# adaLN steps in locked groups with one load each, started behind the RWKV scan, and mLSTM scores copied out of PSUM, in a hybrid DiT layer

## The chip, the cores and the metric

One core of a Trainium2 chip runs the whole layer as one program. The metric is the device time of one execution in microseconds (us); lower is better. TensorE multiplies, VectorE (DVE), ScalarE (ACT) and GpSimd (POOL) work elementwise, SyncE (SP) issues most of the DMA transfers. Each engine works through its own queue in the order in which the program lists it.

## What is computed

One layer of a diffusion backbone on 256 latent and 256 context tokens of width 2048, in fp32. The condition vectors c and c_ctx give, through one matrix w_mod of 2048 x 12288, six modulation vectors (adaLN). Cut to what matters here:

```python
mod_x = (silu(c) @ w_mod + b_mod)[:, None, :]
mod_c = silu(c_ctx) @ w_mod + b_mod
sh1x, sc1x, gt1x, sh2x, sc2x, gt2x = split(mod_x, 6)
ux = modulate(rms_norm(x, norm_g[0]), sh1x, sc1x)      # and uc from ctx
s = split_cols(ux @ w_in)                               # also for uc
ya = conv_module(s[0]);  yb = mlstm(s[1], s[2], s[3])
yc = gated_deltanet(s[4], s[5], s[6]);  yd = rwkv7(s[7])
mx = sum(sigmoid(gates) * stack([ya, yb, yc, yd]) @ w_br) @ w_out
x = x + gt1x * rms_norm(mx, norm_g[1])
fx = conv_ffn(modulate(rms_norm(x, norm_g[2]), sh2x, sc2x))
x = x + gt2x * rms_norm(fx, norm_g[3])
```

The recurrent branches scan the context first, then the latents. The modulation of the first norm (sh1, sc1) is needed at the start, gt1 only after the output projection, sh2 and sc2 only before the FFN, gt2 at the end. The mLSTM has four heads; for each, its scores are k against q, 512 keys by 256 queries, which the decay masks then weigh.

## The kernel before

**Big products.** A weight matrix comes in pieces of 256 rows by 512 columns (512 KB, tile `raw`). `load_split` (L187) loads a piece, ScalarE makes its rounded copy `hi` (L198) and VectorE the rest `lo` (L200); TensorE then takes three products per tile. `mode_b` (psum `psB`) keeps weights stationary, `mode_a` (psum `psA`) keeps activations stationary: 12 matmuls of 128x512 per piece for two token tiles. All matmuls are issued in `mm`, L79, so one line holds them all, and the psum's name tells them apart.

**The adaLN product.** `wmod_steps` (L248) makes one block of 512 columns of `mod` in eight steps. A step loads 512 KB of w_mod into the tile `wraw` of the pool `wmr`, which has one buffer, and issues four fp32 matmuls `psw` (two records each in the trace) that add into one PSUM bank. Then ScalarE copies the sums to `wrows` (L268), and two matmuls `psf` spread them; for the blocks of the gains G1 and G2, which hold gt1 and gt2 times a norm's weight on all partitions, VectorE adds the bias to them (L278, from `wbg`, two loads of 256 KB) and GpSimd multiplies. `mod_feed` lists the blocks: first 8 blocks of sh2 and sc2 (`mod2`), then 4 of G1, then 4 of G2. The blocks of sh1 and sc1 are made in phase 0, at the start, and the G2 blocks in the FFN; both use the ring `raw` instead of `wraw`.

**When the steps are issued.** `feed` is called once per piece of `mode_a` and `mode_b`; it adds `rate` to a counter and issues as many steps as the counter has passed. The rate is 0.55 from the mLSTM's columns on (L1578) through `conv_columns`, the gate columns and `gates`; `feed(96)` (L1596) issues what is left of the first 96 steps (12 blocks). The order of the engines' queues is not that of the code: the tile framework schedules the program by a timeline of its own (`schedule_with_timeline_sim`, L1678), so that steps and column pieces fill in where scans wait. A group of instructions under `manual_schedule` stays together.

**Stages in time.** Phase 0 (norm, sh1 and sc1) to about 134 us, RWKV columns and features to 470, the RWKV scan with columns as filling to about 782, then the dense stage: columns, the RWKV output (psum `psgo`, `psyo`), the DeltaNet scan (`gd_scan`), the gate columns. `ml_scan` (L1175) runs from about 1210 to 1318: per head four matmuls of scores into two PSUM banks `psq`, mask matmuls `psr`, the weighted scores `mA` on VectorE and ScalarE (L1247 to L1267), then `psn` (mA against mv), and a division `mlh` (L1271). The auxiliary psums share three banks (`auxg`, L1584). From 1318 the merges of the four branches follow (`merge`, L1324, with `sig` tiles reloaded from DRAM), the convolution module's norm (`pscm`, `pscv`), `out_proj`, and from 1504 the FFN.

**Memory.** Pools are opened and closed in stack order from both sides of SBUF. `wmr` is opened early (L1565), `gop`, the DeltaNet's output, on the right side before `gd_scan`. `G1` (the tile of `g1p`) is opened behind `ml_scan`.

Of the kernel before, what the change touches and what calls it, by code (L numbers as in the profile page):

```python
# [11 lines left out]
F32 = mybir.dt.float32  # L12
# [8 lines left out]
P = 128  # L21
# [20 lines left out]
class Kern:  # L42
# [205 lines left out]
    def wmod_steps(self, cb, dst, raws=None, gain=None):  # L248


        nc, A = self.nc, self.A
        if raws is not None and cb in (0, 4):
            ps = self.mmp.tile([P, 512], F32, tag="mm", name="psw")
        else:
            ps = (self.evp if self.wap is not None else self.aux)("psw")
        w = A["w_mod"][0]
        for j in range(8):
            wr = raws or self.wmr
            raw = self.raw() if wr is None else wr.tile([P, 2, 512], F32, tag="wraw", name="wraw")
            nc.sync.dma_start(out=raw, in_=w[256 * j : 256 * j + 256, 512 * cb : 512 * cb + 512].rearrange("(k p) c -> p k c", p=P))  # L260
            for k in range(2):
                for h in range(2):
                    r = slice(64 * h + 32 * k, 64 * h + 32 * k + 32)
                    self.mm(ps[r, 0:256], self.cst[:, 2 * j + k, :], raw[:, k, 256 * h : 256 * h + 256], start=(j == 0), stop=(j == 7))
            if j < 7:
                yield
        rows = self.stage("f3", 256, "wrows")
        nc.scalar.activation(rows, ps[:, 0:256], AF.Copy)  # L268
        if gain is not None:

            bg = self.stage("f2", 512, "wbg"), self.stage("f2", 512, "wbg")
            for t, row in zip(bg, (A["b_mod"][0], gain)):
                c0 = 512 * cb if row is not gain else 512 * (cb % 4)
                nc.sync.dma_start(out=t, in_=row[c0 : c0 + 512].unsqueeze(0).to_broadcast([P, 512]))
            ps = (self.evp if self.wap is not None else self.aux)("psf")
            for h in range(2):
                self.mm(ps[:, 256 * h : 256 * h + 256], self.selb[:, h], rows)
            nc.vector.tensor_tensor(dst, ps, bg[0], ALU.add)  # L278
            nc.gpsimd.tensor_tensor(dst, dst, bg[1], ALU.mult)
            yield  # L280
            return
        ps = (self.evp if self.wap is not None and raws is None else self.aux)("psf")
        for i in range(2):
            self.mm(ps[:, 4 * i : 4 * i + 4], rows[:, P * i : P * i + P], self.sel4.rearrange("p h c -> p (h c)"))
        n = dst.shape[2]
        bm = self.PC["b_mod"][:, 4 * cb : 4 * cb + 4].unsqueeze(2).to_broadcast([P, 4, n])
        for h in range(2):
            nc.vector.tensor_tensor(dst[:, 2 * h : 2 * h + 2], ps[:, 0:8].rearrange("p (i h c) -> p h i c", h=2, c=2)[:, h, :, 0:n],
                                    bm[:, 2 * h : 2 * h + 2], ALU.add)
        yield  # L290
# [564 lines left out]
    def conv_module(self):  # L855
        nc, PC = self.nc, self.PC
        cp = self.cvp
        cpad = cp.tile([P, 4, 286], F32, name="cpad")
        nc.gpsimd.memset(cpad[:, :, 0:15], 0.0)
        nc.gpsimd.memset(cpad[:, :, 271:286], 0.0)  # L860
        nc.sync.dma_start(out=cpad[:, :, 15:271], in_=self.dcv)
        acc = cp.tile([P, 4, 256], F32, name="cacc")
        w = lambda i, t: PC["conv_dw"][:, 4 * t + i : 4 * t + i + 1]
        for i in range(4):
            a = acc[:, i]
            nc.vector.tensor_scalar(a, cpad[:, i, 0:256], w(i, 0), PC["conv_b"][:, i : i + 1], ALU.mult, ALU.add)
            for t in range(1, 31):
                nc.vector.scalar_tensor_tensor(a, cpad[:, i, t : t + 256], w(i, t), a, ALU.mult, ALU.add)  # L868
        ps = self.aux("pscm")
        for i in range(4):  # L870
            self.mm(ps[:, 0:256], self.ones, acc[:, i], start=i == 0, stop=i == 3)
        mean = cp.tile([P, 256], F32, tag="cmean", name="cmean")
        nc.scalar.activation(mean, ps[:, 0:256], AF.Copy, scale=1.0 / 512)
        ps2 = self.aux("pscv")
        for i in range(4):
            nc.vector.tensor_tensor(acc[:, i], acc[:, i], mean, ALU.subtract)
            sq = cp.tile([P, 256], F32, tag="ctap", name="csq", bufs=2)
            nc.scalar.activation(sq, acc[:, i], AF.Square)
            self.mm(ps2[:, 0:256], self.ones, sq, start=i == 0, stop=i == 3)
        rt = cp.tile([P, 256], F32, tag="cmean", name="crt")  # L880
        nc.scalar.activation(rt, ps2[:, 0:256], AF.Sqrt, bias=self.eps6, scale=1.0 / 512)
        nc.vector.reciprocal(rt, rt)
        for i in range(4):
            nc.vector.tensor_tensor(acc[:, i], acc[:, i], rt, ALU.mult)
            nc.scalar.activation(acc[:, i], acc[:, i], AF.Silu, bias=PC["conv_ln_b"][:, i : i + 1], scale=PC["conv_ln_g"][:, i : i + 1])
        self.dbg("ya", acc)
        for i in range(4):
            self.put_y(0, i, acc[:, i])
# [120 lines left out]
        for off, ev, t0, n in ((C_GDK, ev_k, 0, 512), (C_GDV, ev_v, 0, 512), (C_GDQ, ev_q, 256, 256)):  # L1009
            self.mode_b(self.win(off, 512), 512, [(P * i, P, t0, n, ev(i)) for i in range(4)], self.uh, self.ul, KT)  # L1010

    def gd_scan(self):
        nc = self.nc
        gp = self.bp
        ges = ExitStack()
        up = self.pool("gup", stack=ges, side="right")
        wp = self.pool("gwp", bufs=2, stack=ges, side="right")
        tp = self.pool("gtp", stack=ges, side="right")
        lg, beta = self.lg, self.beta
        b4 = lambda ap, r=P: ap.unsqueeze(2).to_broadcast([r, 4, P])  # L1020

# [9 lines left out]
        for c in range(2):  # L1031
            r = slice(64 * c, 64 * c + 64)
# [30 lines left out]
        for seg in range(2):  # L1063
# [5 lines left out]
            for jj in range(2):  # L1069
                j = 2 * seg + jj  # L1070
# [12 lines left out]
                for h in range(4):  # L1083
                    for c in range(2):
                        r = slice(64 * c, 64 * c + 64)
# [11 lines left out]
            for i in range(4):  # L1097
# [21 lines left out]
                if seg:  # L1119

                    g = go[:, (0, 1, 1, 0)[i]]
                    pq = v4(self.aux("pQS"))
# [20 lines left out]
        for c in range(2):  # L1143
            r = slice(64 * c, 64 * c + 64)
# [30 lines left out]
    def ml_scan(self):  # L1175
        nc = self.nc
        self.mlx = ExitStack()
        mp = self.pool("mrp", stack=self.mlx)
        wa = self.pool("mwa", bufs=2, stack=self.mlx)
        wp = self.pool("mwb", bufs=2, stack=self.mlx)  # L1180
        qk = self.pool("mqk", stack=self.mlx)
        mqT, mkT = qk.tile([P, 4, 256], F32, name="mqT"), qk.tile([P, 4, 512], F32, name="mkT")
        mv = mp.tile([P, 4, 4, 132], F32, name="mv")
        nc.gpsimd.memset(mv[:, :, :, 128:129], 1.0)
        nc.sync.dma_start(out=mqT, in_=self.dmq)
        nc.sync.dma_start(out=mkT, in_=self.dmk)
# [6 lines left out]
        for d in range(2):  # L1193
            li, lf, b, m = (mp.tile([4, 512], F32, tag="mr%d" % k, name="mr%d" % k) for k in range(4))
            for src, dst in ((self.li, li), (self.lf, lf)):
                ps = self.aux("psml")
# [12 lines left out]
            ps = self.aux("psmt")  # L1209
# [8 lines left out]
            r = mp.tile([4, 256], F32, name="mlr%d" % d)  # L1218
# [17 lines left out]
        for h in range(4):  # L1236
            pq = [self.aux("psq%d" % i) for i in range(2)]
            for j in range(4):
                self.mm(pq[j // 2][:, 256 * (j % 2) : 256 * (j % 2) + 256], mkT[:, h, P * j : P * j + P], mqT[:, h])
            for d in range(2):  # L1240
                pr = self.aux("psr")
                self.mm(pr[:, 0:256], sel[:, h], rr[d])
# [295 lines left out]
    def build(self):  # L1538
# [12 lines left out]
        ues = self.ues = ExitStack()  # L1551
        self.up = self.pool("up", stack=ues)
        bp = self.bp = self.pool("bp", stack=ues)
        self.wmr = self.pool("wmr", bufs=1, stack=ues)
        self.xes = ExitStack()
        self.x2 = self.pool("x2", stack=self.xes)
        fes = ExitStack()
# [17 lines left out]
        self.aux_pool("auxr", u=2, s=1)  # L1575
        self.rw_scan()
        self.gd_columns()
        self.rate = 0.55  # L1578
        self.ml_columns()
        self.conv_columns()  # L1580
        self.gz = self.gate_columns(C_GDZ, AF.Silu, "gz")
# [3 lines left out]
        res.close()  # L1585
        ces = ExitStack()
        cvs = ExitStack()
        self.cvp = self.pool("cvp", stack=cvs, side="right")
        self.gop = self.pool("gop", stack=ces, side="right")
        self.gd_scan()  # L1590
        self.gd_out()
        ces.close()
        self.ml_scan()
        self.G[0] = self.pool("g1p", stack=ues).tile([P, D], F32, name="G1")
        self.gates()
        self.feed(96)  # L1596
        self.rate = 0.0
# [3 lines left out]
        self.dbg("yh", self.uh[:, :, 0:256].bitcast(F32))  # L1601
        self.dbg("yl", self.ul[:, :, 0:256].bitcast(F32))
        self.resp = self.pool("resp", side="right")
        self.hlp = self.pool("hlp", bufs=2, stack=ues)
        self.mgw = self.pool("mgw", bufs=3, stack=ues)
        self.mgp = self.pool("mgp", stack=ues)
        self.mg = self.mgp.tile([P, 2, D], F32, name="mg")
        self.x1 = self.resp.tile([P, 2, D], F32, name="x1")
        self.ffdw = self.resp.tile([P, 404], F32, name="ffdw")
        self.nc.sync.dma_start(out=self.ffdw[:, 0:396], in_=self.A["taps"])  # L1610
# [71 lines left out]
```

## Time and profile before

| | |
|---|---|
| runs (three) | 2315.18, 2315.31, 2319.65 us |
| median | 2315.31 us |
| profiled execution | 2316.15 us, its span 2313.7 us |
| TensorE busy | 2216.0 us, 96% of the span |
| VectorE, ScalarE, GpSimd busy | 1448.9, 990.7, 374.2 us |
| chain of work that ended last | TensorE 83%, VectorE 6%, DMA 5% |
| DMA | 471.97 MB, mean 204 GB/s |

The profile is of one execution. Its stretches are given in us from the span's start. A piece "x8" in the timeline is eight records in a row of one kind; the time in square brackets is how long the engine stood before it, and for what. A busy TensorE may still run at the lower of its two clocks; the granted clock is given per stretch as a share of the full one.

### The profile page before, as it was taken

To read this page: it belongs to the slowest core of one execution; us is meant where nothing else is said; L and a number is where in the kernel's file an instruction comes from. 1 tells how busy PE (TensorE), PEld (TensorE's weight loads), DVE (VectorE), ACT (ScalarE), POOL (GpSimd) and SP (SyncE) were. 2 spreads that over 40 slices of the span, in tenths; PEclk is the share of its full clock that TensorE was granted. 3 is DMA by queue.
4 is the path that set the end of the run, shared out by engine and by line. 5 is a ranking of instruction groups with operands and counts; after the bars stand their busy time and mean duration, and the time that the engine had idled before them with its cause. 6 is when DMAs were issued, how large, how long until landed. Compare 5 with 4: busy or idle time off the path is not lost.

```text
span 2313.7 us, 42812 instructions
## 1 busy us (share of the span) xinstructions
PE 2216.0 (96%) x16828; PEld 1810.1 (78%) x16828; DVE 1448.9 (63%) x3089; ACT 990.7 (43%) x1498; POOL 374.2 (16%) x739
## 2 busy tenths in 40 slices
PE   6988899999999999999999899989999999999998
PEld 3657677877888776677777678779999999988886
DVE  3356766744555698457564486477776677775554
ACT  4225554533454344344244344344433444444443
POOL 0012453433455021010000042010000000000000
PEclk8999999999999999999999899989999999999999
DMA  9934663555665777776786576567776666665552
GB/s 370 346 124 123 176 185 104 169 164 157 200 201 179 243 245 245 229 236 208 217 268 205 175 277 199 190 216 221 220 219 216 202 183 183 182 205 197 192 192 99
DMA packets 273867, 471.97 MB, mean 204 GB/s; under 512 B 41761, under 2 KB 80929, under 8 KB 272673
## 3 DMA queue, kind: packets, MB, share of 16 engines
q1 hardware_dynamic: 273378, 467.14, 65.0%
q8 instruction: 132, 2.16, 0.4%
q10 hardware_dynamic: 288, 2.10, 0.2%
q14 instruction: 69, 0.57, 0.1%
HBM read 440.33 MB, written 28.84 MB: 203 GB/s over the span
## 4 chain that ended last, share of the span: by engine, by line
PE 83%; DVE 6%; DMA 5%; ACT 2%; issue 1%; POOL 1%; SPq 0%; DVEq 0%; ACTq 0%; POOLq 0%
PE psB L79 38%; PE psA L79 21%; PE psD L79 10%; PE psw L79 4%; DMA wraw<-in_w_mod 3%; DVE lo L200 2%; DMA raw<-in_w_mix 1%; PE psG L79 1%; DVE cacc L868 1%; ACT hi L198 1%; PE psn L79 1%; PE psf L79 1%; PE psSA L79 1%; PE psY L79 0%; PE pd L79 0%
## 5 line engine op out<-in xcount | busy, mean ns | idle before, releaser
L200 DVE TENSOR_TENSOR lo<-raw,hi 128x1024 fp32r<-128x1024 f32 (+2 forms) x485 | 594.1, 1226 | 462.3 <-ACT hi L198 457.0
L198 ACT ACTIVATE hi<-raw 128x1024 fp32r<-128x1024 f32 (+2 forms) x488 | 508.5, 1043 | 804.3 <-PE psB L79 368.4
L79 PE MATMUL psB<-u2h,lo 128*128 128x256 f32 x1408 | 397.4, 284 | 0.0
L79 PE MATMUL psB<-u2l,hi 128*128 128x256 f32 x1408 | 397.1, 283 | 0.3 <-DVE u2l L1364 0.3
L79 PE MATMUL psB<-u2h,hi 128*128 128x256 f32 x1408 | 396.0, 286 | 1.2 <-DVE u2h L1363 1.2
L79 PE MATMUL psA<-lo,uh 128*128 128x512 f32 x832 | 335.5, 404 | 5.5 <-DVE lo L200 5.4
L79 PE MATMUL psA<-hi,ul 128*128 128x512 f32 x832 | 330.0, 397 | 0.0
L79 PE MATMUL psA<-hi,uh 128*128 128x512 f32 x832 | 309.9, 403 | 6.1 <-ACT hi L198 3.9
L79 PE MATMUL psB<-uh,hi 128*128 128x256 f32 (+1 forms) x832 | 280.9, 346 | 18.5 <-ACT hi L198 16.2
L79 PE MATMUL psB<-ul,hi 128*128 128x256 f32 (+2 forms) x832 | 278.9, 339 | 0.0
L79 PEld LDWEIGHTS psB<-u2h,hi 128*128 128x128 f32 x1408 | 268.0, 193 | 10.9 <-issue 9.5
L79 PE MATMUL psB<-uh,lo 128*128 128x256 f32 (+2 forms) x832 | 263.5, 340 | 8.4 <-DVE lo L200 8.4
L79 PEld LDWEIGHTS psB<-u2l,hi 128*128 128x128 f32 x1408 | 270.4, 192 | 0.5 <-DVE u2l L1364 0.5
L79 PEld LDWEIGHTS psB<-u2h,lo 128*128 128x128 f32 x1408 | 270.3, 192 | 0.1
L79 PEld LDWEIGHTS psA<-lo,uh 128*128 128x128 f32 x832 | 156.9, 189 | 54.1 <-DVE lo L200 10.2
L79 PEld LDWEIGHTS psB<-uh,hi 128*128 128x128 f32 x832 | 158.4, 191 | 51.0 <-ACT hi L198 18.3
L79 PEld LDWEIGHTS psA<-hi,uh 128*128 128x128 f32 x832 | 153.9, 189 | 54.8 <-issue 14.6
L79 PEld LDWEIGHTS psA<-hi,ul 128*128 128x128 f32 x832 | 157.0, 189 | 35.6 <-issue 2.0
L79 PEld LDWEIGHTS psB<-uh,lo 128*128 128x128 f32 (+1 forms) x832 | 153.2, 190 | 32.4 <-DVE lo L200 10.9
L79 PEld LDWEIGHTS psB<-ul,hi 128*128 128x128 f32 (+1 forms) x832 | 158.2, 190 | 23.3 <-issue 6.2
L1534 DVE TENSOR_TENSOR lo<-raw,hi 128x1024 fp32r<-128x1024 f32 x88 | 107.6, 1225 | 79.8 <-ACT hi L1533 79.7
L1454 DVE SCALAR_TENSOR_TENSOR facc<-fpad,ffdw,facc 128x256 f32<-128x256 f32 x352 | 152.9, 488 | 0.2
(570 smaller groups left out, 2903.8 us busy)
## 6 DMA issues: line engine op xcount, KB each, us to landing
raw<-in_w_in SPq DMA_DIRECT2D x208, 512.0 KB, 4.6
raw<-in_ffn_up SPq DMA_DIRECT2D x176, 512.0 KB, 3.8
wraw<-in_w_mod SPq DMA_DIRECT2D x160, 512.0 KB, 5.3
raw<-in_ffn_down SPq DMA_DIRECT2D x88, 512.0 KB, 4.5
raw<-in_w_br SPq DMA_DIRECT2D x32, 512.0 KB, 5.3
raw<-in_w_out SPq DMA_DIRECT2D x32, 512.0 KB, 4.6
raw<-in_w_mod SPq DMA_DIRECT2D x32, 512.0 KB, 3.8
raw<-in_w_in SPq DMA_DIRECT2D x48, 256.0 KB, 4.0
```

What stands on the lines that cost most here:

```text
L79: self.nc.tensor.matmul(out, lhsT, rhs, start=start, stop=stop)
L198: nc.scalar.activation(hi[s], raw[s], AF.Copy)
L200: (nc.gpsimd if self.pool_lo >= 0 else nc.vector).tensor_tensor(lo[s], raw[s], hi[s].bitcast(F32), ALU.subtract)
L868: nc.vector.scalar_tensor_tensor(a, cpad[:, i, t : t + 256], w(i, t), a, ALU.mult, ALU.add)
L1454: nc.vector.scalar_tensor_tensor(s3(acc), pad[:, dy : dy + 4, dx : dx + 64], tap(t, b), s3(acc), ALU.mult, ALU.add)
L1534: nc.vector.tensor_tensor(f(lo), f(raw), f(hi).bitcast(F32), ALU.subtract)
```

## The change

Outside phase 0 and the FFN, a block's eight steps now share three loads: three steps, three and two, of 1.5, 1.5 and 1 MB, into a `wraw` tile three times as large, still with one buffer. The matmuls of such a group, 12, 12 and 8, are issued together under `manual_schedule`, at high priority. (Steps of phase 0 and of the FFN are locked in fours.) The pool `wmr` is opened only behind `rw_out`, so no step can use it beside the RWKV scan, and the rate is set to 0.76 only before `gates`. In `ml_scan` a head's scores are copied from their two banks into an SBUF tile `msc`, one half by VectorE, one by ScalarE, and the masks are applied to that. The other edits are of memory: `gop` moves into `gd_scan` and to the left side, the mLSTM's pools change their order and split, the convolution's squares are written into `cpad` in place of a tile of their own, and `hlp` is opened later.

```diff
 def wmod_steps(self, cb, dst, raws=None, gain=None):
...
+        alone = raws is not None or self.wmr is None
+        starts = range(8) if alone else (0, 3, 6)
         for j in range(8):
-            wr = raws or self.wmr
-            raw = self.raw() if wr is None else wr.tile([P, 2, 512], F32, tag="wraw", name="wraw")
-            nc.sync.dma_start(out=raw, in_=w[256 * j : 256 * j + 256, 512 * cb : 512 * cb + 512].rearrange("(k p) c -> p k c", p=P))
-            for k in range(2):
-                for h in range(2):
-                    r = slice(64 * h + 32 * k, 64 * h + 32 * k + 32)
-                    self.mm(ps[r, 0:256], self.cst[:, 2 * j + k, :], raw[:, k, 256 * h : 256 * h + 256], start=(j == 0), stop=(j == 7))
+            if j in starts:
+
+                j0, n = j, 1 if alone else min(3, 8 - j)
+                raw = self.raw() if alone and raws is None else (raws or self.wmr).tile([P, 2 if alone else 6, 512], F32, tag="wraw", name="wraw")
+                nc.sync.dma_start(out=raw[:, 0 : 2 * n], in_=w[256 * j : 256 * (j + n), 512 * cb : 512 * cb + 512].rearrange("(k p) c -> p k c", p=P))
+            if j == j0 + n - 1:
+                with self.tc.manual_schedule(engines={mybir.EngineType.PE}), ExitStack() if alone else self.tc.high_priority():
+                    for k in range(2 * n):
+                        kt = 2 * j0 + k
+                        for h in range(2):
+                            r = slice(64 * h + 32 * (k % 2), 64 * h + 32 * (k % 2) + 32)
+                            self.mm(ps[r, 0:256], self.cst[:, kt, :], raw[:, k, 256 * h : 256 * h + 256], start=(kt < 2), stop=(kt > 13))
             if j < 7:
                 yield
...
 def conv_module(self):
-            sq = cp.tile([P, 256], F32, tag="ctap", name="csq", bufs=2)
+            sq = cpad[:, i, 0:256]
...
 def gd_scan(self, ces):
+        self.gop = self.pool("gop", stack=ces)
...
 def ml_scan(self):
+        qk = self.pool("mqkv", stack=self.mlx)
+        wa = self.pool("mwa", bufs=2, stack=self.mlx)
         mp = self.pool("mrp", stack=self.mlx)
-        wa = self.pool("mwa", bufs=2, stack=self.mlx)
+        wq = self.pool("mwq", stack=self.mlx)
         wp = self.pool("mwb", bufs=2, stack=self.mlx)
-        qk = self.pool("mqk", stack=self.mlx)
...
-        mv = mp.tile([P, 4, 4, 132], F32, name="mv")
+        mv = qk.tile([P, 4, 4, 132], F32, name="mv")
...
+            sc = wq.tile([P, 2, 512], F32, tag="sc", name="msc")
+            for i in range(2):
+                self.evac(sc[:, i], pq[i], "act" if i else "dve")
+            pq = [sc[:, i] for i in range(2)]
...
 def build(self):
-        self.wmr = self.pool("wmr", bufs=1, stack=ues)
...
-        self.rate = 0.55
         self.ml_columns()
...
+        self.wmr = self.pool("wmr", stack=ues)
         self.cvp = self.pool("cvp", stack=cvs, side="right")
-        self.gop = self.pool("gop", stack=ces, side="right")
-        self.gd_scan()
+        self.gd_scan(ces)
         self.gd_out()
         ces.close()
         self.ml_scan()
         self.G[0] = self.pool("g1p", stack=ues).tile([P, D], F32, name="G1")
+        self.rate = 0.76
         self.gates()
         self.feed(96)
...
-        self.hlp = self.pool("hlp", bufs=2, stack=ues)
         self.mgw = self.pool("mgw", bufs=3, stack=ues)
         self.mgp = self.pool("mgp", stack=ues)
         self.mg = self.mgp.tile([P, 2, D], F32, name="mg")
+        self.hlp = self.pool("hlp", bufs=2, stack=ues)
```

How the order of the queues changes, at three places. First TensorE in the DeltaNet scan, in the dense stage (`pc`, `pd` are its small matmuls, `psA` a column's), before:

```order
L79 MATMUL pc<-giTD,gN 32x32 x16
L79 MATMUL psw<-wraw,cst 32x256 x4
```

and now:

```order
L79 MATMUL pd<-giD_9491,giM_9529 32x32
L79 MATMUL psA<-hi,uh 128x512 x2
L79 MATMUL psw<-wraw,cst 32x256 x12
L79 MATMUL pd<-giD_9491,giM_9529 32x32 x15
L79 MATMUL psA<-lo,uh 128x512
```

A step of four matmuls between other work has become a group of three steps. Between the start of the RWKV scan and the end of the mLSTM 96 steps stood in 109 runs, 60 of them between two column matmuls; now 72 stand there in 27 runs, 10 of them between two.

Second, TensorE from the mLSTM's last head (`psr`, `psn`) to the first merge (the first `psA` after it), before:

```order
L79 MATMUL psw<-wraw,cst 32x256 x4
L79 MATMUL psf<-wrows,selb 128x256 x2
L79 MATMUL psn<-mv,mA 128x129 x7
L79 MATMUL psr<-mlr_11030,mlsel 128x256 x2
L79 LDWEIGHTS idb
L79 MATMUL psr<-mlmask,idb 128x256
L79 MATMUL psn<-mv,mA 128x129 x7
L79 MATMUL psA<-hi,uh 128x512
```

and now:

```order
L79 MATMUL psn<-mv,mA 128x129 x12
L79 MATMUL psw<-wraw,cst 32x256 x24
L90 MATMUL psho<-ident,mlh 128x128 x8
L79 MATMUL pscm<-cacc,ones 128x256 x4
L79 MATMUL psw<-wraw,cst 32x256 x8
L79 MATMUL pscv<-cpad,ones 128x256
L79 MATMUL psf<-wrows,selb 128x256 x2
L79 MATMUL pscv<-cpad,ones 128x256 x3
L79 MATMUL psw<-wraw,cst 32x256 x32
L79 MATMUL psf<-wrows,selb 128x256 x2
L79 MATMUL psw<-wraw,cst 32x256 x32
L79 MATMUL psf<-wrows,selb 128x256 x2
L79 MATMUL psA<-hi,uh 128x512
```

Three whole blocks, 24 steps, have moved between the mLSTM's last `psn` and the first merge, with `psho`, `pscm` and `pscv`, which stood among the merges. Their loads on SP, now (before, none of w_mod stood behind the mLSTM's end ahead of the FFN's):

```order
L264 DMA wraw<-in_w_mod 128x6x512
L264 DMA wraw<-in_w_mod 128x4x512
L1344 DMA sig<-dg_11354 128x1024 x2
L264 DMA wraw<-in_w_mod 128x6x512
L1344 DMA sig<-dg_11354 128x1024
```

Of eight such loads these are the first three.

Third, VectorE where the first G1 block is added, before, in the DeltaNet scan:

```order
L96 COPY gU<-pd 32x8x32
L278 TENSOR_TENSOR G_11353<-psf,wbg 128x512
L1114 SCALAR_TENSOR_TENSOR gX<-pKS,gmnegc,gV 128x128 x4
```

and now, in the mLSTM's last head:

```order
L1284 TENSOR_SCALAR mlh<-psn,dn 128x128 x2
L285 TENSOR_TENSOR G_11350<-psf,wbg 128x512
L1280 TENSOR_TENSOR dn<-dn,mlem 128x2
```

The add has moved from the DeltaNet scan to between the divisions of the last head.

## Rows read from the trace of the kernel before

**Rows 1.** The page: span, and busy time of each engine.

```profile
span 2313.7 us, 42812 instructions
PE 2216.0 (96%) x16828; PEld 1810.1 (78%) x16828; DVE 1448.9 (63%) x3089; ACT 990.7 (43%) x1498; POOL 374.2 (16%) x739
```

**Rows 2.** Stretches: us; PE, PEld, DVE, ACT, POOL busy; PEclk, DMA share, GB/s.

```profile
782.00:1057.00 275.00, 268.92 (x1964) 192.00 (x1961) 206.38 (x516) 113.97 (x145) 34.00 (x41) 1.00 0.80 245
...
1511.00:1515.00 4.00, 3.24 (x24) 0.60 (x24) 3.45 (x15) 2.81 (x9) 0.00 (x0) 0.50 1.05 396
```

**Rows 3.** Timeline of TensorE around one step, dense stage: start, us, piece.

```profile
1042.82 0.40 PE L79 MATMUL psA<-hi,ul 128*128 128x512 f32 x1
1043.15 0.64 PE L79 MATMUL psw<-wraw,cst 128*32 128x256 f32 x8
1043.71 0.74 PE L79 MATMUL psA<-hi,uh 128*128 128x512 f32 x2
1044.29 0.40 PE L79 MATMUL psA<-lo,uh 128*128 128x512 f32 x1
```

**Rows 4.** Stretches, psw alone, 470 to 1318 us: the sum.

```profile
sum 848.00, PE 69.31 PEld 16.80 ACT 4.59; mean PE 17.33 PEld 4.20 ACT 1.15
```

**Rows 5.** Timeline of TensorE at the FFN's first steps.

```profile
1503.97 2.37 PE L79 MATMUL psw<-raw,cst 128*32 128x256 f32 x40
1511.05 1.08 PE L79 MATMUL psw<-raw,cst 128*32 128x256 f32 x8 [4.72 <-DMA raw<-in_w_mod]
```

**Rows 6.** Waits of TensorE, 470 to 1345 us: total, times, longest.

```profile
PE psw L79 <- DMA wraw<-in_w_mod: 4.2, 8, 1.0
PE psA L79 <- DVE lo L200: 3.6, 5, 1.7
```

**Rows 7.** The tile wraw, 782 to 1057 us: its loads.

```profile
DMA to landing us min/median/max: 3.6/4.9/7.7
```

**Rows 8.** Chain that ended last, around one load: start, us, piece.

```profile
1031.02 5.76 DMA wraw<-in_w_mod
...
1036.83 0.64 PE psw L79 x8
1037.47 5.75 PE psA L79 x24
```

**Rows 9.** Timeline of TensorE, end of the mLSTM.

```profile
1302.57 0.64 PE L79 MATMUL psw<-wraw,cst 128*32 128x256 f32 x8 [0.61 <-DMA wraw<-in_w_mod]
1303.93 1.64 PE L79 MATMUL psf<-wrows,selb 128*128 128x256 f32 x4 [0.73 <-ACT wrows L268]
...
1312.80 3.35 PE L79 MATMUL psn<-mv,mA 128*128 128x129 f32 x14 [1.74 <-ACT mA L1252]
1318.24 0.80 PE L79 MATMUL psA<-hi,uh 128*128 128x512 f32 x1 [2.09 <-DVE mg L1337]
```

**Rows 10.** Groups of ScalarE: a PSUM tile of 128x512 read; busy, mean ns.

```profile
L1319 ACT ACTIVATE sig<-psA 128x512 f32<-128x512 f32 x32 | 19.0, 599 | 25.2 <-PE psA L79 25.1
```

**Rows 11.** DMA issues: KB each, median us to landing.

```profile
raw<-in_w_mod SPq DMA_DIRECT2D x32, 512.0 KB, 3.8
...
xt<-in_ctx SPq DMA_DIRECT2D x2, 1024.0 KB, 6.7
xt<-in_x SPq DMA_DIRECT2D x2, 1024.0 KB, 13.0
...
x<-in_x ACTq DMA_DIRECT2D x2, 1024.0 KB, 7.6
```

**Rows 12.** Timeline of TensorE in the first merges.

```profile
1329.46 0.82 PE L90 MATMUL psho<-ident,mlh 128*128 128x128 f32 x6
1333.10 1.89 PE L79 MATMUL pscm<-cacc,ones 128*128 128x256 f32 x8
1344.01 1.02 PE L79 MATMUL pscv<-csq,ones 128*128 128x256 f32 x4
1353.62 0.73 PE L79 MATMUL psA<-hi,uh 128*128 128x512 f32 x2 [3.04 <-ACT hi L198]
```

More of the change, by code (lines that the diff above doesn't have):

```diff
@@ L1010, in gd_columns, with gd_scan @@
             self.mode_b(self.win(off, 512), 512, [(P * i, P, t0, n, ev(i)) for i in range(4)], self.uh, self.ul, KT)
-    def gd_scan(self):
+    def gd_scan(self, ces):
         nc = self.nc
```

## The prediction

> **What bounds the kernel now.** I read the page first: TensorE is busy 96% of the span and no other engine over 63% [rows 1], so time is made or lost in TensorE's queue, which runs in the order that the program lists. The profiled execution took 2316.15 us beside its span of 2313.7; the median of the three runs is 2315.31. I make the sum as a difference on that span and add it to the median.
>
> Then the stretches [rows 2]. From 782 to 1057 us, the dense stage (column matmuls, DeltaNet scan, RWKV output), TensorE is busy 268.9 of 275 us, and the DMA engines move 245 GB/s at a share of 0.80: a fifth is to spare, not more. From 1511 to 1515 us, little but w_mod steps ran: 396 GB/s at a share of 1.05, and the granted clock was 0.50, the lower level (1.2 GHz); TensorE had stood 4.72 us just before [rows 5].
>
> What one step costs TensorE stands in the timeline [rows 3]. From 1042.82 to 1044.29 us, 1.47 us, lie three steps from psA to psA, which take 0.24 us each elsewhere (x24 in 5.75 us [rows 8]), and one w_mod step: it costs 1.47 - 3 x 0.23 = 0.78 us. In a long run a further step costs (2.37 - 0.64) / 4 = 0.43 us, by the x40 piece against the x8 one (two records per matmul, so x8 is one step) [rows 3, 5]. The other 0.35 us is the switch: I put 0.14 to the run itself (its own 0.57 against 0.43) and 0.21 to the matmuls around it where both are column matmuls. The trace's busy time of psw from 470 to 1318 us is 69.3 us [rows 4].
>
> The waits are few: from 470 to 1345 us, 4.2 us for wraw in eight pieces and 3.6 for lo [rows 6]. The single wraw buffer shows in the chain: a load of 5.76 us ends, and its step starts 0.05 us later [rows 8]. Landing takes 3.6 to 7.7 us, median 4.9 [rows 7].
>
> **Part 1, switches saved.** In the old order, 96 steps stand between the RWKV scan's start and the mLSTM's end, in 109 runs, 60 of them between two column matmuls: 96 x 0.43 + 109 x 0.14 + 60 x 0.21 = 69.1 us, the busy time of [rows 4]. In the new order 72 steps lie there, in 27 runs, 10 between two column matmuls: 72 x 0.43 + 27 x 0.14 + 10 x 0.21 = 36.8. That is -32 us. Three psf pairs leave with the other 24 steps, 0.8 us each by [rows 9] (1.64 for two), of which I count 0.5: **-34 us**. The column matmuls done by the mLSTM's end are the same in both orders (1776 psA of 2496). The RWKV scan, which loses its w_mod steps as filler, gets columns instead: by its end the new order has 139 more psA in place of 131 psw.
>
> **Part 2, the dense stage.** All 72 steps now lie between the RWKV scan's end and the second half of the DeltaNet scan, where 40 were. Old: 275 us x 245 GB/s = 67.4 MB [rows 2]. New: 32 more steps (+16.8 MB) and 119 fewer psA, so 10 fewer 512 KB column loads (-5.2): 79 MB. TensorE's work there becomes 268.9 - 119 x 0.24 + 11 = 251 us, which asks 315 GB/s, a share of 0.80 x 315 / 245 = 1.03. What a 1.5 MB load takes, no row shows. Lower end: the loads stay hidden and the 6.1 idle us go: -6. Upper end: each of 27 loads, 4.9 + 2.6 = 7.5 us (1 MB more at 396 GB/s), is held up by a further 2 us at that share; the gaps between groups are 5.6 to 11.7 us by their column matmuls at 0.24, so most groups would wait 1 to 2 us: +30. I take **+8 us**, since the mean gap, 251 / 27 = 9.3 us, is longer than 7.5, and only the shorter third stalls.
>
> **Part 3, mLSTM heads.** The score copies (two of 128x512 a head) cost about 0.6 us each on ACT by its copy of that shape [rows 10], VectorE's I take alike. They free two PSUM banks before the head's masks and lie beside columns except in the last head, where the old order stands 0.61 to 1.74 us at a time [rows 9]. From -6 (three of those stands go) to +4 (each head's copies delay it): **-3 us**. The csq square in cpad's place and the order of the pools change nothing that TensorE waits for: 0, covered by the merges' columns.
>
> **Part 4, the tail.** Behind the mLSTM's last psn the new order has 24 steps, the last three G1 blocks, before the first merge psA. VectorE's rows say why: a G1 block's add now stands between the last head's divisions, because, as I read it, G1 takes space that the mLSTM gives back. What covered these steps, the columns, is used up by then. One load is ahead; eight come one by one through the one buffer (five of 1.5 MB, three of 1 MB), each behind the group before it; on SP, which issues them, sig reloads and the bias rows queue behind each. Price of a load, lower end: 512 KB on a quiet queue took 3.8 us [rows 11], at least 3.6 [rows 7]; with 2.6 for 1 MB and 1.3 for 512 KB more at 396 GB/s [rows 2], 6.2 and 4.9. Upper end: 1 MB took 6.7 to 7.6 [rows 11] (13.0 at the program's start, among many other loads, which this tail is not), so 7.6, and 9.8 for 1.5 MB (7.6 and 1.7 times 1.3). Groups: a step took 1.08 us at the lower clock [rows 5] and 0.43 to 0.64 at the full one, so 2.8 and 2.0 against 1.4 and 1.0 us. Low: 5 x 6.2 + 3 x 4.9 + 8 x 1.25 = 56, and 3 for the first group and psf; high: 5 x 9.8 + 3 x 7.6 + 8 x 2.5 = 92 and 6. From 59 to 98, I take 70, near the low end, as little else loads there (four sig reloads of 512 KB, six 256 KB rows). It stands in place of the 2.1 us wait for mg [rows 9]: **+68 us**.
>
> The Trainium skill (DMA: Bandwidth & Descriptors, section Anatomy of one DMA) states about 2 us fixed and then bytes over 436 GB/s; an estimate by that page is 5.6 and 4.4 us a load, so 41 us for the eight where the rows give 46 to 72, and a tail of 54 to 67 us. It would move the sum to some +20, not the sign.
>
> **Part 5, behind the tail.** From the first merge psA, 1318.24 [rows 9], to the FFN's first w_mod step, 1503.97 [rows 5], are 185.7 us. The 3.0 us wait for hi at 1353.62 goes, as hi has time to be made in the tail; psho, pscm and pscv, 0.8 + 1.9 + 1.0 us, are in the tail now [rows 12]; the restart at the lower clock costs about 1: **-6 us** (from -12, with lo's waits gone too, to +5, should the weight buffers not be filled ahead).
>
> **Sum.** -34 + 8 - 3 + 68 - 6 = +33: 2315.3 + 33 = **2348 us**.
>
> **Rivals.**
> *Larger loads pay (faster).* For it: waits for wraw exist [rows 6], and three 512 KB loads in flight moved 396 GB/s. If a 1.5 MB load lands about like a 512 KB one under load (4.4 us, between 3.8 and 4.9), the tail is 8 x (4.4 + 1.25) = 45, and with parts 2, 3 and 5 at their low ends: -34 - 6 - 6 + 43 - 12 = -15, **2300 us**. With those ends it decides once the tail is under 55 us, with the parts as I took them under 32. Against: one buffer, so nothing of a load lies beside the group ahead of it. Chance 0.13. The Trainium skill (the same page, section Bandwidth) says to batch DMAs to 1 MiB or more, which is this rival's mechanism; the runs of before have no such load with a twin of 512 KB to show it.
> *No change.* Tail at 59, the other parts at their low ends: -34 - 6 - 6 + 57 - 12 = -1, **2314 us**. Chance 0.07.
> *DMA-bound dense stage.* Part 2 at +30 and a tail of 75: +60, **2375 us**. For it: the share of 1.03 that the stage would need; against: 1.05 does occur [rows 2]. Chance 0.14.
> *The change doesn't do what it says*, with groups split or copies that still hold the banks: the order shows 12, 12 and 8 whole, so a few us at most, inside the forecast. Chance 0.01.
>
> **How the numbers follow.** The forecast, slower by 15 to 50 us, has 0.65. Slower in all 0.65 + 0.14 + 0.01 = 0.80; within 0.2% (4.6 us, about what a measurement of this kernel tells from no change) 0.07; faster 0.13. The range, 2302 to 2382, leaves out about half of the first rival and the worse half of the third, and some of the forecast's own ends.
>
> **What would show it.** Right: psw busy near 37 us up to the mLSTM's end; behind the last psn eight waits of psw for wraw, 4 to 8 us each, with a granted clock near 0.5; the FFN's first step about 33 us later. Wrong: waits under 4 us there, or a dense stage with long waits for hi, lo and wraw.

## The result, and the profile after

The changed kernel takes 2352.4 us (median of four runs, 2349.1 to 2355.82), the kernel before beside it 2315.24: a ratio of 1.0162, 95% interval 1.0143 to 1.0181, or 37 us more. The prediction said 2348 (2302 to 2382), slower with a chance of 0.80.

On the page of the changed kernel, the span, TensorE's busy time, and its row and the granted clock's in the 40 slices (tenths):

```profile
span 2347.2 us, 42724 instructions
PE 2197.8 (94%) x16828; PEld 1817.0 (77%) x16828; DVE 1448.5 (62%) x3093; ACT 985.3 (42%) x1496; POOL 375.0 (16%) x739
...
PE   6979889999999998999998389989999999999998
...
PEclk8989999999999999999999689989999999999999
```

TensorE works 18 us less than before and the span is 33.5 us longer [rows 1], so 51.7 us more of it are idle. The slices show where: the 23rd, from 1291 us on, is 3 tenths busy at 0.6 of the clock. That is where the mLSTM has ended and the merges, which add up the four branches, have not begun.

The timeline of TensorE there (start, us, piece, in brackets what it waited for):

```profile
1283.64 1.17 PE L79 MATMUL psn<-mv,mA 128*128 128x129 f32 x8
1285.60 1.50 PE L79 MATMUL psw<-wraw,cst 128*32 128x256 f32 x24 [0.78 <-DVE G L285]
1295.78 2.79 PE L79 MATMUL psw<-wraw,cst 128*32 128x256 f32 x24 [8.68 <-DMA wraw<-in_w_mod]
...
1303.84 1.07 PE L79 MATMUL psw<-wraw,cst 128*32 128x256 f32 x16 [1.11 <-DMA wraw<-in_w_mod]
...
1312.34 2.79 PE L79 MATMUL psw<-wraw,cst 128*32 128x256 f32 x24 [4.50 <-DMA wraw<-in_w_mod]
1325.96 2.79 PE L79 MATMUL psw<-wraw,cst 128*32 128x256 f32 x24 [10.83 <-DMA wraw<-in_w_mod]
1333.77 1.93 PE L79 MATMUL psw<-wraw,cst 128*32 128x256 f32 x16 [5.03 <-DMA wraw<-in_w_mod]
...
1342.13 2.79 PE L79 MATMUL psw<-wraw,cst 128*32 128x256 f32 x24 [3.85 <-DMA wraw<-in_w_mod]
1351.43 2.79 PE L79 MATMUL psw<-wraw,cst 128*32 128x256 f32 x24 [6.51 <-DMA wraw<-in_w_mod]
1359.46 1.93 PE L79 MATMUL psw<-wraw,cst 128*32 128x256 f32 x16 [5.24 <-DMA wraw<-in_w_mod]
...
1366.82 0.79 PE L79 MATMUL psA<-hi,uh 128*128 128x512 f32 x1 [2.85 <-DVE mg L1350]
```

This is the tail: one group whose load was ahead, eight that wait for theirs, 45.8 us of waiting in all. Seven of the eight groups run at the lower clock, in 2.79 and 1.93 us (2.8 and 2.0 had been worked out); one ran at the full clock, in 1.07 us. From the last psn's end (1284.81) to the first merge psA are 82.0 us, where the kernel before had 2.1 [rows 9]. The tail takes more than the whole loss; the rest of the kernel gained 46 us.

Where it gained, in three views of the changed kernel. The stretches, psw alone, up to the mLSTM's end (us; PE, PEld, ACT busy; granted clock, DMA share, GB/s):

```profile
470.00:1285.00 815.00, 37.28 (x576) 16.46 (x576) 3.47 (x9) 1.00 0.66 205
```

The stretches in the dense stage, all engines, and in the tail where TensorE waits longest (columns as in [rows 2]):

```profile
786.00:1020.00 234.00, 218.55 (x1820) 159.40 (x1819) 168.18 (x408) 83.22 (x111) 26.45 (x32) 0.99 0.89 290
...
1315.00:1327.00 12.00, 1.17 (x16) 0.58 (x16) 0.00 (x0) 0.00 (x0) 0.00 (x0) 0.50 0.81 306
```

The waits of TensorE from 470 to 1262 us (us in total, times, longest), and the landing of wraw's loads from 780 to 1060:

```profile
PE psw L79 <- DMA wraw<-in_w_mod: 11.9, 8, 3.2
PE psA L79 <- DVE lo L200: 4.7, 6, 1.5
```

```profile
DMA to landing us min/median/max: 5.2/7.1/10.4
```

psw's busy time fell from 69.3 to 37.3 us [rows 4], its waits before the tail rose from 4.2 to 11.9 [rows 6], and the last psn ends 31.3 us earlier (1284.81 against 1316.15 [rows 9]). The FFN's first steps in the timeline of TensorE:

```profile
1542.79 2.37 PE L79 MATMUL psw<-raw,cst 128*32 128x256 f32 x40
1547.36 0.64 PE L79 MATMUL psw<-raw,cst 128*32 128x256 f32 x8 [2.21 <-DMA raw<-in_w_mod]
```

Behind the tail the way to the first of them is 175.97 us (1366.82 to 1542.79) instead of 185.73, and from there to the end 804.4 instead of 809.7. So -31.3 + 79.9 - 9.8 - 5.3 = +33.5, the difference of the spans.

### The profile page after: what moved, and what is told of

It is laid out like the page before. It is cut to its first block, busy times and chain, and to the rows that moved or that the text cites. A ratio compares the mean times of both kernels' runs of the same rounds, so it can differ in the third digit from the quotient of the medians.

```text
span 2347.2 us, 42724 instructions
## 1 busy us (share of the span) xinstructions
PE 2197.8 (94%) x16828; PEld 1817.0 (77%) x16828; DVE 1448.5 (62%) x3093; ACT 985.3 (42%) x1496; POOL 375.0 (16%) x739
## 4 chain that ended last, share of the span: by engine, by line
PE 78%; DMA 8%; DVE 7%; ACT 2%; issue 2%; POOL 2%; SPq 0%; DVEq 0%; POOLq 0%; ACTq 0%
PE psB L79 35%; PE psA L79 20%; PE psD L79 10%; DMA wraw<-in_w_mod 6%; PE psw L79 3%; DVE lo L200 2%; DVE cacc L875 1%; DMA raw<-in_w_mix 1%; POOL riU L410 1%; ACT hi L198 1%; PE psG L79 1%; POOL rim L409 1%; PE psn L79 1%; DVE ribs L441 0%; PE pKS L79 0%
## 5 line engine op out<-in xcount | busy, mean ns | idle before, releaser
L79 PEld LDWEIGHTS psA<-lo,uh 128*128 128x128 f32 x832 | 157.1, 189 | 50.2 <-DVE lo L200 11.6
L79 PE MATMUL psw<-wraw,cst 128*32 128x256 f32 x1280 | 97.6, 427 | 78.0 <-DMA wraw<-in_w_mod 77.0
```

The source lines that it names most:

```text
L79: self.nc.tensor.matmul(out, lhsT, rhs, start=start, stop=stop)
```

## The experiments

Each kernel below is the changed kernel with the edit shown, unless it says otherwise; the kernel before, beside them, had medians of 2313.05 (e1 to e4) and 2313.31 us (e5 to e8), 2 us under the 2315.24 beside the changed kernel; a difference from the changed kernel is uncertain by about that much. None leaves out part of the computation.

The theory was that a memory overlap, not the groups, makes the tail: in the built program the tile G1 (opened behind `ml_scan`) lies on the bytes of the mLSTM's weighted scores mA, so the G1 blocks can't be finished before the last head is. VectorE's timeline of the changed kernel bears this out: the add of the first G1 block reads only psf and wbg, but starts when the last psn, which reads mA, has ended (1284.81):

```profile
1284.85 0.69 DVE L285 TENSOR_TENSOR G<-psf,wbg 128x512 f32<-128x512 f32 x1 [1.00 <-PE psn L79]
```

### e1: without the copies

```diff
-            sc = wq.tile([P, 2, 512], F32, tag="sc", name="msc")
-            for i in range(2):
-                self.evac(sc[:, i], pq[i], "act" if i else "dve")
-            pq = [sc[:, i] for i in range(2)]
```

> The changed kernel without the copies of the mLSTM's scores (the masks are applied to PSUM as before); groups of three steps, one buffer and the tail of 24 steps stay as they are. Theory (the tail of uncovered steps is the loss, the copies hardly matter): 2352 us, 2346 to 2358, the stretch from the last psn to the first merge psA again near 82 us, and the mLSTM's heads at most 4 us longer. Rival (the copies bring much of what the mLSTM's end gained, last psn 31 us earlier): 2360 us or more. Rival (the copies cost): under 2346 us.

Measured: 2365.93 us (2362.56 to 2368.59), 13.5 more than the changed kernel. The last psn ends at 1300.3 us instead of 1284.8, and the tail is what it was (80.9 us):

```profile
1296.95 3.35 PE L79 MATMUL psn<-mv,mA 128*128 128x129 f32 x14 [1.79 <-ACT mA L1261]
...
1381.17 0.76 PE L79 MATMUL psA<-hi,uh 128*128 128x512 f32 x1 [2.84 <-DVE mg L1346]
```

The waits of TensorE from 1200 to 1301 us:

```profile
PE psn L79 <- ACT mA L1261: 7.1, 4, 1.8
PE psr L79 <- DVE mlh L1280: 2.9, 2, 1.5
PE psr L79 <- DVE mlh L1282: 0.6, 1, 0.6
```

My expectation of "at most 4 us longer" fell, and the rival (2360 us or more) came. In this order the columns are used up before the last heads, which then run on their own chain. The copies hide most of it: the changed kernel has a single 1.7 us wait there. So TensorE is idle 8.4 us longer by its last psn. The other 7.1 of the 15.5 us are busy time (801.01 against 793.95 us from 470 us on): from 1270 to 1300 us the granted clock is 0.57 and then 0.72, where the changed kernel had 0.88 from 1270 to its last psn.

### e2: G1 in a place of its own

As e1, and:

```diff
-            sq = pool.tile([P, nh, w], F32, tag=tag + "sq", name=tag + "sq")
+            sq = pool.tile([P, nh, w], F32, tag="mr0" if tag == "mh" else tag + "sq", name=tag + "sq")
...
-            yf = pool.tile([P, 256], F32, tag=tag + "yf", name=tag + "yf", bufs=2)
+            yf = pool.tile([P, 256], F32, tag=tag + "yf", name=tag + "yf", bufs=1 if tag == "mh" else 2)
```

> As e1, and the mLSTM's output norm saves 3 KB (its square tile takes the place of an earlier one, one buffer less), so that G1 gets space of its own at the top instead of the masks' tile mA: all 96 steps, still in groups of three, two and one load each, then stand before the mLSTM's last psn, in 36 runs, and none behind it. Theory (the tail comes from G1's place and costs 80 us, the groups themselves gain): psw before the last psn 96 x 0.43 + 36 x 0.14 + 12 x 0.21 = 49 us against 69 of the kernel before; no tail; waits for wraw in the dense stage up to 15 us; so 2315 - 20 + 8 - 5 (the FFN's start) = 2298 us, 2285 to 2312. Rival (large loads through one buffer cost in the dense stage what the switches gain; the tail would just be paid there): 2315 to 2350 us, with waits of psw for wraw of 30 us and more before the last psn.

Measured: 2325.39 us (2323.34 to 2329.5), 40.5 less than e1. The tail of steps is gone and psw's busy time is 50.2 us, as worked out (49). All four G1 blocks are now added before the last psn ends (VectorE, first and last start):

```profile
L285 DVE TENSOR_TENSOR G<-psf,wbg x4: 672/678/692, 1177.3 to 1281.6; 128x512 f32<-128x512 f32 x4
```

But it is 27 us more than my forecast and 13 above its range, and the kernel is slower than the one before (ratio 1.006, interval 1.0039 to 1.008). The timeline of TensorE at the mLSTM's end says why:

```profile
1307.86 3.35 PE L79 MATMUL psn<-mv,mA 128*128 128x129 f32 x14 [1.79 <-ACT mA L1261]
1318.73 1.54 PE L90 MATMUL psho<-ident,mlh 128*128 128x128 f32 x6 [7.53 <-DVE mlh L807]
...
1321.94 3.78 PE L79 MATMUL pscm<-cacc,ones 128*128 128x256 f32 x8 [0.82 <-DVE mhyf L817]
1327.10 3.68 PE L79 MATMUL pscv<-cpad,ones 128*128 128x256 f32 x8 [1.38 <-ACT cpad L885]
1338.22 0.80 PE L79 MATMUL psA<-hi,uh 128*128 128x512 f32 x1 [7.44 <-DVE mg L1346]
```

Another 27 us pass before the first merge, though no w_mod step is left. The rival (large loads pay for themselves in the dense stage) was not it: waits of psw for wraw are 12.3 us, not 30. With G1 at the top, the merges' sum mg has come to lie on the convolution's cpad and cacc, so the first merge waits for the convolution's norm, which waits behind the mLSTM's output norm on VectorE. That this is a matter of mg's place, e5 tests.

### e5: mg in a place of its own too

As e2, and:

```diff
-        self.resp = self.pool("resp", side="right")
-        self.mgw = self.pool("mgw", bufs=3, stack=ues)
         self.mgp = self.pool("mgp", stack=ues)
+        self.mgw = self.pool("mgw", bufs=3, stack=ues)
+        self.resp = self.pool("resp", side="right")
```

> As e2 (no copies, G1 in a place of its own), and the pools of the merges are opened in another order (mg, then sig, then x1), so that mg no longer takes the place of the convolution's tiles cpad and cacc; x1, written much later, does. Theory (in e2 the first merge waited for the convolution's norm through mg's place, 27 us from the last psn to the first merge psA against 2 in the kernel before): that stretch falls to 2 to 5 us, with psho, pscm and pscv among the merges again, some 20 us in all: 2325 - 20 = 2305 us, 2297 to 2312. Rival (the merge waits for the mLSTM's output norm or the convolution by VectorE's order, wherever mg lies): 2318 us or more.

Measured: 2302.26 us (2301.05 to 2306.89), 23 less than e2. The same place in the timeline:

```profile
1304.26 3.35 PE L79 MATMUL psn<-mv,mA 128*128 128x129 f32 x14 [1.79 <-ACT mA L1261]
1311.15 0.80 PE L79 MATMUL psA<-hi,uh 128*128 128x512 f32 x1 [3.54 <-DVE mg L1346]
1319.35 0.82 PE L90 MATMUL psho<-ident,mlh 128*128 128x128 f32 x6
```

3.5 us to the first merge instead of 27, and psho among the merge's matmuls again. Not all of the 23 us is this: 6 of them lie behind the FFN's first step (809.9 us from there to the end in e2, 803.9 here), where this edit explains nothing.

### e6: the whole change without the overlaps

As e5 with the copies back, and the gate tile of the mLSTM's output norm in the copies' place:

```diff
-        wq = self.pool("mwq", stack=self.mlx)
+        wq = self.mwq = self.pool("mwq", stack=self.mlx)
...
-        g = pool.tile([P, 4, 256], F32, name=tag + "g")
+        g = self.mwq.tile([P, 4, 256], F32, tag="sc", name=tag + "g") if tag == "mh" else pool.tile([P, 4, 256], F32, name=tag + "g")
```

> As e5, and with the copies of the scores (the gate tile of the mLSTM's output norm shares the copies' tile, so that G1 still has its own place): the whole change without its two overlaps of tiles. Theory (the copies shorten the mLSTM's heads by the 13 us that e1 lost without them): 2305 - 10 = 2295 us, 2285 to 2303, last psn 8 us or more before that of e5. Rival (the copies pay only where no columns cover the heads): as e5 within 4 us.

Measured: 2294.24 us (2292.67 to 2299.64), ratio 0.992 (0.9897 to 0.9944). It beats both kernels: 19 us less than the kernel before, 58 less than the changed one. The copies give 8 us here. (Of the 19 us, 5.5 lie behind the FFN's first step, as in the changed kernel; see below.)

### e7: single steps in three buffers, without the overlaps

As e6, and:

```diff
-        starts = range(8) if alone else (0, 3, 6)
+        starts = range(8)
...
-                j0, n = j, 1 if alone else min(3, 8 - j)
+                j0, n = j, 1
...
-        self.wmr = self.pool("wmr", stack=ues)
+        self.wmr = self.pool("wmr", bufs=3, stack=ues)
```

(and the tile is [P, 2, 512], so the memory is the same).

> As e6, but single steps, 512 KB each, in three buffers of a third of the size; its order has 75 runs of psw instead of 36. Theory (what the groups gain is the switch, 0.14 us a run and 0.21 between column matmuls): 39 runs more, some 25 of them between columns, is 5 + 5 = 10 us more than e6, less the waits that one large buffer makes in the dense stage (12 us in e2): within 6 us of e6, 2290 to 2303. Rival (grouping is the gain): 10 us or more above e6. Rival (one large buffer is the loss): 8 us or more below e6.

Measured: 2294.21 us (2293.75 to 2299.48), e6's time within 0.1 us. Switches and waits are both there and cancel: psw's busy time from 470 to 1370 us, of e6 and of e7 (the first figure behind the length),

```profile
470.00:1370.00 900.00, 49.58 (x768) 21.98 (x768) 4.64 (x12) 0.99 0.69 220
```

```profile
470.00:1370.00 900.00, 56.99 (x768) 17.16 (x768) 4.55 (x12) 0.99 0.69 220
```

and the waits of TensorE from 470 to 1380 us, of e6 and of e7:

```profile
PE psw L79 <- DMA wraw<-in_w_mod: 11.9, 10, 2.2
```

```profile
PE psw L79 <- DMA wraw<-in_w_mod: 3.1, 5, 0.9
```

Groups save 7.4 us of psw over single steps (39 runs fewer) and lose 8.8 us in its waits, because one buffer has to be read before it can be filled. Over everything from 470 us to the last psn, TensorE is busy 808.1 us in e6 and 820.0 in e7, and idle 20.9 and 9.2: 11.9 against 11.7 us. This compares size and number of buffers together; large loads in several buffers would need more memory and were not tried.

### e3: single steps in three buffers, with the overlaps

The edit of e7 on the changed kernel.

> The changed kernel with single steps (512 KB loads, four matmuls together) in three buffers of a third of the size, so the same memory; 24 steps again behind the last psn. Theory (the tail's price is the single buffer: each load waits for the group before it): loads overlap, 12.6 MB at about 396 GB/s is 32 us, with the steps of the last block a tail of 36 to 48 us instead of 82; against that 61 runs instead of 31 cost some 10 us of switches; 2352 - 40 + 10 = 2322 us, 2312 to 2332. Rival (the tail is set by what the DMA engines can move or by bias rows and sig reloads in SP's queue): tail over 65 us and 2345 us or more.

Measured: 2334.64 us (2332.95 to 2335.0), between the theory's 2332 and the rival's 2345; the tail is 66.5 us (1286.41 to 1352.91), on the rival's side:

```profile
1352.91 0.79 PE L79 MATMUL psA<-hi,uh 128*128 128x512 f32 x1 [2.85 <-DVE mg L1350]
```

With three buffers the tail's waits of psw for wraw are 27.4 us instead of 45.8. Two neighbouring rows of the timeline show that loads now arrive in a row (0.21), but that some are late all the same (8.12):

```profile
1317.88 1.08 PE L79 MATMUL psw<-wraw,cst 128*32 128x256 f32 x8 [0.21 <-DMA wraw<-in_w_mod]
1327.08 1.08 PE L79 MATMUL psw<-wraw,cst 128*32 128x256 f32 x8 [8.12 <-DMA wraw<-in_w_mod]
```

The single buffer is thus about a fifth of the tail's price (82.0 to 66.5 us), less than half of what the theory gave it (82 to between 36 and 48). Two things stay in either kernel. Two loads of x, 1 MB each, go out on ScalarE's queue in the middle of it: in the changed kernel's timeline of ScalarE and in its stretch from 1315 to 1327 us (above), 306 GB/s for 12 us is 3.7 MB, which is about one 1.5 MB load and both of x, and that load takes 10.7 us.

```profile
1314.48 0.87 ACTq L1426 DMA_DIRECT2D x<-in_x  x2
```

And each block ends with wrows, psf, the add and the product before the bias buffers are free for the next; in the changed kernel's chain that ended last:

```profile
1335.77 0.39 ACT wrows L275
...
1336.21 2.09 PE psf L79 x4
...
1338.32 0.70 DVE G L285
...
1339.09 1.27 POOL G L286
```

How much each of the two is worth alone was not tried.

### e4: single steps, one buffer

`starts = range(8)`, a tile [P, 2, 512] and one buffer: the late start without groups and large loads. The copies stay.

> The changed kernel with single steps (512 KB, four matmuls together) and one buffer of a third of the size: the late start alone, without groups and large loads. Its order has 94 runs, 21 steps behind the last psn, 7 of them before the first merge psA. Theory (groups gain by fewer switches, the late start brings the tail): switches saved shrink from 32 us to 5 or so, the tail to some 7 steps of 6 us and two psf, about 45 us, and the rest beside the merges: 2315 - 5 + 45 - 10 = 2345 us, 2325 to 2365. Rival (the late start is harmless, large loads make the loss): 2315 us or less.

Measured: 2332.5 us (2327.89 to 2338.91), ratio 1.009 (1.0065 to 1.0115). With one small buffer the late start is a loss: 21 of the 96 steps are left at the mLSTM's end, 7 of them before the first merge, and the stretch to it, from 1297.10 to 1329.38, is 32 us:

```profile
1295.27 1.83 PE L79 MATMUL psn<-mv,mA 128*128 128x129 f32 x14
...
1329.38 0.80 PE L79 MATMUL psA<-hi,uh 128*128 128x512 f32 x1
```

The rival (late start harmless, large loads the loss) is out for this form of it. But e6 and e7 start just as late and gain, so the late start by itself is not the loss either. And it is not the overlap of the changed kernel: the first G1 add stands at 1280.18 here, before the last psn. That one small buffer is too slow for the late start is argued from the order, not shown by a run that changes nothing else.

### e8: the copies in the kernel before

On the kernel before: the copies of e1's diff added, their tile sharing the gate tile's place.

> The kernel before with the copies of the mLSTM's scores alone (in the gate tile's place); its adaLN steps are where they were, but one that its order now puts behind the last psn. Theory (the copies free PSUM banks and so let the heads run ahead): last psn 5 to 12 us earlier and 2303 to 2311 us. Rival (beside the steps and columns of the old order the heads are covered anyway): 2311 to 2317 us. Rival (the copies cost): above 2317.

Measured: 2309.93 us (2305.59 to 2313.03), ratio 0.9979 (0.9966 to 0.9993), -3.4 us. The last psn ends some 12 us earlier, but the output norm's psho then stands 5.6 us for mlh, uncovered:

```profile
1302.04 1.73 PE L79 MATMUL psn<-mv,mA 128*128 128x129 f32 x14
...
1313.78 1.54 PE L90 MATMUL psho<-ident,mlh 128*128 128x128 f32 x6 [5.60 <-DVE mlh L800]
```

What the copies give early is partly paid there.

## Why the prediction was right, point by point

**The mechanism** was the forecast's: a tail of steps behind the mLSTM that costs more than the switches give back. That the sum (+33) meets the difference of the spans (+33.5; the medians differ by 37) is luck: the tail was forecast 11.9 us too small, and three other stretches, -2.3, -3.8 and -5.3 us, make up for it. Of the signs that were named, psw's 37 us and the eight waits came, the waits from 1.1 to 10.8 us instead of 4 to 8, at a granted clock of 0.50 from 1312 to 1340 us but 0.87 in the 14 us before. The FFN's first step is 38.8 us later, not 33.

**Part 1, switches (-32 and 2 of psf).** Right. The busy time of psw up to the last psn is 37.3 us, 36.8 were worked out. The same prices (0.43 a step, 0.14 a run, 0.21 between column matmuls) give 49.5 and 49.0 for e2 and e6, which took 50.2 and 49.6 in 36 runs, but 59.8 for e7, which took 57.0 in 75: they are somewhat too high for many runs. How the 0.35 us of a switch divides into 0.14 and 0.21 was a choice.

**Part 2, dense stage (+8).** Right: psw waits 11.9 instead of 4.2 us, loads land in 7.1 us where 7.5 had been estimated. The DMA engines moved 290 GB/s at a share of 0.89, below the 315 at 1.03 that I had asked of them; over TensorE's busy 218.6 us of those 234 alone it would be 310, so the waits stretch the stage by about what is missing. The rival of a stage bound by the DMA engines is out: e7 moves 313 GB/s there at a share of 0.95 with fewer waits.

**Part 3, mLSTM heads (-3).** Mis-sized. The copies are worth 13.5 us in the changed kernel (e1), 8 in e6, 3.4 in the kernel before (e8). I had priced the copies against the heads' waits in the old order, where columns fill them. In the new order the columns come earlier and the heads at the end stand alone; e1 shows that as 10.6 us of waits and a lower clock. Parts 1 to 3 were forecast at -29 and came to -31.3, as the waits that I hadn't seen and the copies that remove them lie in the same stretch. By TensorE's time from 470 us to the last psn, busy fell by 40.9 us (834.85 to 793.95) and idle rose by 9.6; psw is 32.0 of the first and psf about 3, and what the rest is made of was not followed up.

**Part 4, the tail (+68).** Right in place and mechanism, 12 us too small: 82.0 us, where 59 was the low end of the working. The 23 us above that end are three things. The eight loads took 54 us instead of 46, most of it in two of them: the two loads of x, 2 MB, that the new order sends there (the kernel before sends them at 1358 us, among the merges) were not in my list of what loads there, and the load beside them took 10.7 us; the first load took 8.3 us, with a bias row beside it. Seven groups of eight ran at the lower clock: about 19 us for the eight instead of 10. And the ends of the tail, in front of the first load and behind the last group, are 8 us instead of 3, as wrows, psf, the add, the product and mg follow one another there. Where little else loads, 1 MB landed in 4.9 to 5.2 us and 1.5 MB in 6.2 to 6.4, near the low end of 4.9 and 6.2. The cause that I named with "as I read it", G1 on the mLSTM's bytes, is shown by e2: the same steps, groups and loads, 40.5 us less. By the Trainium skill (DMA: Bandwidth & Descriptors, section Anatomy of one DMA), whose figures are for loads that GpSimd issues, 4.4 and 5.6 us a load is the estimate; these loads, which SP issues, are 0.5 to 0.8 us above it where little else loads.

**Part 5 (-6).** -9.8: the waits for hi and lo fell from 6.2 to 2.1 us, and TensorE's busy time by 5.7 (179.4 to 173.8), as all of psho, pscm and pscv had moved into the tail; I had counted 18 of their 24 records, by rows that show only some of them.

**Not in the sum.** From the FFN's first step to the end the kernel is 5.3 us shorter. Only 1.8 us of that lie in the FFN's start, up to its first copy into fpad, and they are not simply the wait there: it is 2.2 us instead of 4.7 [rows 5], but e5 to e7 wait 5.1 to 5.3 us again and reach that copy as early. The other 3.7 us lie in the last product (psum psD, the same 1056 matmuls). There the kernel before ran its first 5 us at a granted clock of 0.73, this one at 1.00; and at the full clock its matmuls follow each other a little faster. A stretch of 50 us in the middle of it, before and now (columns as in [rows 2]):

```profile
2095.00:2145.00 50.00, 50.00 (x220) 41.04 (x219) 26.07 (x28) 22.04 (x28) 0.00 (x0) 1.00 0.57 191
```

```profile
2130.00:2180.00 50.00, 50.00 (x222) 41.39 (x222) 26.43 (x28) 22.20 (x28) 0.00 (x0) 1.00 0.60 195
```

The product takes 244.1 us in the kernel before, e4 and e8, 240.4 in the changed kernel, e3, e5, e6 and e7, and 241.8 and 242.7 in e1 and e2. Why is open; nothing that was tried separates it, and one profile of each kernel doesn't say how much of it is chance.

**The rivals.** "Larger loads pay" needed a tail under 55 us, "no change" one of 59 with every other part at its low end; it was 82.0. The change did what it says: the groups stand whole in the timeline (x24, x16). The rule of the first rival, batches of 1 MiB and more in the Trainium skill (the same page, section Bandwidth), gives nothing here within the same memory: e6 with 1.5 MB in one buffer and e7 with 512 KB in three take the same time.

## What to carry to other kernels

Where tiles share memory, a tile that is opened for a later stage inherits the end of whatever lay there before; giving one tile a place of its own was worth 40 us here, and opening three pools in another order up to 23. Look in the order of the queues for work that has slipped past its cover, and then ask which bytes its output waits for, before judging the groups or loads that were the point of the change. One large buffer or several small ones is a trade of switches against waits, and in this kernel it came out even.

## What the runs showed that I had not expected

That a copy out of PSUM can pay: two copies of 128x512 a head, about 0.6 us on ScalarE and 0.7 on VectorE, took 13.5 us off a chain of four heads once no column matmuls lay beside them (e1), and 3.4 us where they did (e8). And that single steps in three buffers and groups in one are even: 11.9 us of TensorE's busy time against 11.7 us of idle time (e6, e7).
